# Gate stores of a hybrid encoder layer: issued by ScalarE's queue instead of SyncE's

## Chip, cores and metric

The kernel runs on one NeuronCore of one Trainium2 chip. The metric is the time on the device in microseconds (us) of one execution; the number compared is the median over several executions. Engines are named as in the profile: PE is TensorE's matmuls, PEld its weight loads, DVE is VectorE, ACT is ScalarE, POOL is GpSimd, SP is SyncE. A name with a q (SPq, ACTq) is the sequencer of that engine, where it waits or issues a transfer.

## The reference, cut to what matters

One encoder layer is applied to two batches with the same weights: a prompt of 512 tokens and a sample of 1024 tokens, both 1024 wide, all in float32.

```python
def encoder_layer(x, norm_g, w_in, qn_a, kn_a, rpb_a, qn_b, kn_b, sink_b, w_o_a, w_o_b, w_out, t5_table):
    h = rmsnorm(x, norm_g)
    proj = h @ w_in
    qa, ka, va, za, qb, kb, vb, zb, ga, gb = jnp.split(proj, np.cumsum(SPLITS)[:-1], axis=-1)
    ...
    oa = neighbourhood_attention(qa, ka, va, rpb_a) * jax.nn.silu(za)
    oa = oa @ w_o_a
    ...
    ob = window_gqa_attention(qb, kb, vb, t5_table, sink_b) * jax.nn.silu(zb)
    ob = ob @ w_o_b
    merged = jax.nn.sigmoid(ga) * oa + jax.nn.sigmoid(gb) * ob
    return x + merged @ w_out
```

The two gates sigmoid(ga) and sigmoid(gb), each 1024 wide, are what most of the stores in question hold.

## The kernel before, in words

**Arithmetic.** Every matrix is split into a high and a low part (`split`, L1168: ScalarE makes the rounded high part, VectorE or GpSimd the difference), and every product is three matmuls: high by high, low by high, high by low. That is why nearly all work lies on PE.

**Stages.** In order of time: norm and attention of the prompt (up to about 222 us), the dense stage of the prompt (to about 400 us), attention of the sample (to about 790 us), the dense stage of the sample (to the end). A dense stage (`dense_phase`, L1139) computes z (with silu, times the attention result: `post_z`, L1524), the gates ga and gb (sigmoid: `post_gate`, L1587), the two branch products with the merge, and the output projection. Tiles are 128 partitions by 512 columns, 256 KB each. In the sample's dense stage pairs of columns go through Strassen's scheme (`pair_strassen`, L1349), in the prompt's through plain products (`pair_classic`, L1332).

**What goes through memory outside the core.** SBUF can't hold the gates until the merge, so they are stored to `g_d` and loaded again (L1729). The products of silu(z) with attention go through `u_d` in the sample. All these stores are recorded by one helper, `store` (L1518), whose transfer is issued on L1520:

- kind "u" (`post_z`): the tile is the product that VectorE or GpSimd made last.
- kind "g" from `post_gate`: the tile `C`, on which ScalarE has just applied sigmoid (L1513).
- kinds "g" and "p" from `fill_gates` (L1592): some gate products are computed early, between the matmuls of the attention stages, to fill gaps of PE. Their result leaves PSUM by `leave` (L1612, copy on L1616) into the tile `fc`, of which there is one. The copy may be done by ScalarE or by VectorE: the planner chooses. "p" is the first Strassen product, kept in `p_d` and loaded on L1389.

**What sets the order.** The program is not written in the order in which it runs. Each step is recorded as an operation (`op`, L162) with a choice of engines and a cost in ns on each, a priority, the operations it must follow and the buffers it takes. `run` (L207) then plays a list scheduler over these costs: whenever an engine is free in its model, it takes the ready operation with the smallest priority number, and emits its instructions. So the costs fix the order on every engine's queue, in which instructions then run strictly in turn. A transfer is an operation on SP:

```python
    def dma(self, emit, nbytes, prio, **kw):
        return self.op((("sp", 470),), lambda e: emit(), prio, lag=nbytes / 360, **kw)
```

It takes 470 ns of SP in the plan, and `lag` is the transfer itself. All transfers of the kernel are issued by SP. The priority of the early gate work is -5 for stores, ahead of everything else of the stage.

Of the kernel before, what the change touches and what calls it, by code (L numbers as in the profile page):

```python
# [140 lines left out]
class Flow:  # L141
# [45 lines left out]

    def dma(self, emit, nbytes, prio, **kw):
        return self.op((("sp", 470),), lambda e: emit(), prio, lag=nbytes / 360, **kw)

    def stage(self, prio, close=(), open=(), make=()):

        ends = [o for o in self.ops if any(v.args[0] in close for v in o.vals)]
        for v in make:
            v.held = True

        def emit(e):
            for p in close:
                p.close()
            for p in open:  # L200
                p.open()
            for v in make:
                v.make()

        return self.op((("sp", 0),), emit, prio, after=ends)
# [149 lines left out]
def encoder_kernel(  # L355
# [23 lines left out]
    nc = tc.nc  # L379
    act = nc.scalar  # L380
# [51 lines left out]
    f = Flow(pspool)  # L432
# [706 lines left out]
    def dense_phase(geo, hh, hl, h_ops, o_stores, exps_done, start, opened, tp, up, p0, p1, p2, x_t, y_t, classic, fill, after_gates=None, side=None):  # L1139
# [21 lines left out]
        dma = f.dma  # L1161
# [74 lines left out]
        def stored_sums(prio, d, after):  # L1236

            tv, ops = {}, {}
            for j in (1, 2, 0, 3):
                tv[j] = tuple(f.value(tp, [P, 4, nh], F32R, "T", 8) for _ in range(2))  # L1240
                vh, vl = tv[j]
                for k in range(4):
                    st = spare(("fh", "w32")[k // 2]) if not short and d is t_d and k % 2 else tile_("U", 4)
                    dma(
                        lambda st=st, j=j, k=k: nc.sync.dma_start(st.t[:, :nh], d[j, k]), 512 * nh, prio, new=[st],
                        after=[*after(j, k), *([opened] if d is t_d else [])],
                    )
                    ops[j, k] = split(
                        lambda vh=vh, k=k: vh.t[:, k], lambda vl=vl, k=k: vl.t[:, k], lambda st=st: st.t[:, :nh], nh, prio,
                        (vh, k == 0), (vl, k == 0), [st],  # L1250
                    )
            return moving_sums(tv, ops)


        def load_raw(src, prio):
            v = tile_("raw", 4, 512)
            dma(lambda: nc.sync.dma_start(v.t, src), 262144, prio, new=[v], after=[start])
            return v
# [58 lines left out]
        def weight_sums(i, raw, ends, prio):  # L1317
            o = None
            for j, out, in0, in1, op in (
                (2, (1, 1), (1, 0), (1, 1), ALU.add), (1, (1, 0), (0, 0), (1, 0), ALU.subtract),  # L1320
                (0, (0, 0), (1, 1), (0, 0), ALU.subtract), (3, (0, 1), (0, 1), (0, 0), ALU.subtract),
            ):
                v, a, b = raw[out], raw[in0], raw[in1]
                o = tt(
                    lambda v=v: v.t, lambda a=a: a.t, lambda b=b: b.t, op, 512, prio, hold=[v, a, b],
                    after=[*ends, *([o] if o else [])],
                )
                s_saves[i, j] = dma(
                    lambda v=v, j=j: nc.sync.dma_start(s_d[i, j], v.t), 262144, prio, after=[o], hold=[v],
                )  # L1330
# [185 lines left out]
            return sg  # L1516

        def store(kind, key, dst, v, n, prio):  # L1518
            stores.setdefault((kind, *key), []).append(
                dma(lambda: nc.sync.dma_start(dst, v.t[:, :n]), 512 * n, prio, use=[v])  # L1520
            )


        def post_z(c, a, n, v, in_psum, prio):  # L1524
            sg = sigmoid(v, n, prio, not in_psum, AF.Silu)
            m = n // nb
            ots = [tile_("ot", n_ot) for _ in range(2 if c >= 4 else 1)]
            for e, ot in enumerate(ots):
                if c < 4:
                    src, dst = o_d[nt][e, c, :, a : a + n], lambda ot=ot: ot.t[:, :n]  # L1530
                else:
                    src = o_d[nt][e, c].rearrange("p (i n) -> p i n", n=P)[:, :, a // nb : a // nb + m]
                    dst = lambda ot=ot: ot.t[:, :n].rearrange("p (i n) -> p i n", n=m)
                dma(
                    lambda dst=dst, src=src: nc.sync.dma_start(dst(), src), 512 * n, prio - 0.5, new=[ot],
                    after=o_stores[c, a // nh],
                )
            ot, ov, sv = ots[0], lambda: ots[0].t[:, :n], lambda: sg.t[:, :n]
            if len(ots) > 1:
                tt(ov, ov, lambda: ots[1].t[:, :n], ALU.add, n, prio, use=ots, into=[ot])  # L1540
            if c < 4:
                tt(sv, sv, ov, ALU.mult, n, prio, use=[sg, ot], into=[sg])
            else:
                gv = lambda: sv().rearrange("p (n i) -> p n i", n=m)
                tt(gv, gv, lambda: ov().rearrange("p (i n) -> p n i", n=m), ALU.mult, n, prio, use=[sg, ot], into=[sg])
            if short:
                split_u(c, a, n, sg, prio)
            else:
                store("u", (c, a // nh), u_d[c, :, a : a + n], sg, n, prio)
# [37 lines left out]
        def post_gate(br, m, a, n, v, in_psum, prio):  # L1587
            store("g", (br, m, a // nh), g_d[br, m, :, a : a + n], sigmoid(v, n, prio, not in_psum), n, prio)
# [3 lines left out]
        def fill_gates(prio):  # L1592
# [5 lines left out]
            for br, m in filled if short else filled[::2]:  # L1598
# [13 lines left out]
                def leave(ps, kind, key, dst):  # L1612
                    v = f.value(wpool, [P, nh], F32, "fc", 1)
                    o = f.op(
                        (("act", ACT_(nh, False)), ("dve", DVE_(nh))),
                        lambda e, v=v, ps=ps: act.activation(v.t, ps.t, AF.Copy) if e == "act" else dve.tensor_copy(v.t, ps.t),  # L1616
                        soon, new=[v], use=[ps], port=False,
                    )
                    store(kind, key, dst, v, nh, prio)
                    return o  # L1620
# [22 lines left out]
        for i in range(0 if short else 4):  # L1643
# [5 lines left out]
                use=[ps],  # L1649
# [58 lines left out]
        for q in range(8):  # L1708
            m = q if short else q // 2 + 4 * (q % 2)
            prio = 12 + q  # L1710
# [4 lines left out]
            for n in halves:  # L1715
                gs_ = []
                for br in range(2):
# [14 lines left out]
                    if (br, m) in filled and (short or (m % 2, n) == (0, 0)):  # L1732
# [3 lines left out]
                        use=[ps, g], into=[g],  # L1736
# [213 lines left out]
```

## Time and profile before

| | |
|---|---|
| median of 3 runs | 1136.74 us (1136.4 to 1139.61) |
| the profiled execution | 1139.25 us, of it 1137.5 us in the profile's span |
| granted TensorE clock, mean over the span | 0.998 |
| stores issued on L1520 | 72: 34 `g_d<-C`, 14 `g_d<-fc`, 8 `p_d<-fc`, 16 `u_d<-C` |
| moved by all transfers | 186.11 MB, mean 164 GB/s |

The profile is one execution. Its views are: busy time by engine, busy time of each engine in chosen stretches of the span (a table by stage), who waited for whom (a row has the waiting engine and line, what ended the wait, the total in us, how many times, and the longest), the chain of waits that ended last, the instructions in order of time, and the instructions of one line. An issue of a transfer isn't counted as busy time of its engine. Matmuls overlap, so the duration of one (0.39 us for 512 columns) is longer than the distance from one start to the next.

### The profile page before, as it was taken

What the parts mean: (1) busy time and instruction counts of PE and PEld (TensorE: products, weight loads), DVE (VectorE), ACT (ScalarE), POOL (GpSimd) and SP (SyncE); (2) the same over time, 40 slices, a digit from 0 to 9 for tenths busy, and PEclk for the clock granted to TensorE, in tenths of its full rate; (3) what the DMA queues carried; (4) which work ended last, traced back from release to release, by engine and by line L of the source; (5) the groups of instructions that cost most, each with busy time, mean ns of one, the idle gap of its engine ahead of it and who ended that gap; (6) DMA issues with size and microseconds to landing.
All of it is one profiled execution on the core that took longest, in us unless ns stands there. A gap on an engine that the chain in (4) does not pass through costs nothing.

```text
span 1137.5 us, 18703 instructions
## 1 busy us (share of the span) xinstructions
PE 1121.8 (99%) x6079; PEld 975.1 (86%) x6079; DVE 856.8 (75%) x1988; ACT 651.4 (57%) x1499; POOL 339.3 (30%) x438
## 2 busy tenths in 40 slices
PE   8999999999999999999999999999999999999998
PEld 6999988888888889999999988988788888888877
DVE  5878797587776568787878889876988766767564
ACT  5777987644532247565769888877543435333430
POOL 3654433000011144434324343510333323123111
PEclk9999999999999999999999999999999999999999
DMA  7854543488785743121213214244888645756862
GB/s 257 273 159 138 185 115 103 107 254 257 246 286 202 249 138 91 29 61 29 82 41 93 73 38 119 50 131 138 288 261 237 206 158 191 278 197 224 262 208 93
DMA packets 139108, 186.11 MB, mean 164 GB/s; under 512 B 29897, under 2 KB 68561, under 8 KB 139010
## 3 DMA queue, kind: packets, MB, share of 16 engines
q1 hardware_dynamic: 139010, 184.91, 51.8%
q8 instruction: 48, 0.79, 0.3%
q14 instruction: 50, 0.41, 0.1%
HBM read 137.66 MB, written 51.92 MB: 167 GB/s over the span
## 4 chain that ended last, share of the span: by engine, by line
PE 90%; DMA 4%; DVE 2%; ACT 1%; issue 1%; SPq 1%; POOL 0%; ACTq 0%; DVEq 0%
PE p L764 26%; PE x L1293 8%; PE x L1295 8%; PE x L1294 8%; PE x L1066 5%; PE x L1029 5%; PE x L937 5%; PE p L1294 4%; PE p L1295 4%; PE p L1293 4%; PE d L1293 4%; PE d L1295 4%; PE d L1294 4%; PE x L864 2%; DMA w<-in_w_att_dram 1%; DMA U<-m_d 1%
## 5 line engine op out<-in xcount | busy, mean ns | idle before, releaser
L764 PE MATMUL p<-whi,hh 128*128 128x384 f32 x384 | 133.7, 348 | 0.0
L764 PE MATMUL p<-whi,hl 128*128 128x384 f32 x384 | 132.6, 345 | 0.0
L764 PE MATMUL p<-wlo,hh 128*128 128x384 f32 x384 | 132.0, 344 | 0.0
L1172 ACT ACTIVATE whi<-raw 128x512 fp32r<-128x512 f32 (+1 forms) x140 | 81.5, 600 | 73.0 <-PE x L1294 22.5
L981 ACT ACTIVATE sb<-sb,mx 128x384 f32<-128x384 f32 (+1 forms) x192 | 107.7, 565 | 16.9 <-DVE mx L972 16.6
L1294 PE MATMUL x<-T,whi 128*128 128x512 f32 x280 | 108.9, 389 | 0.0
L1293 PE MATMUL x<-T,whi 128*128 128x512 f32 x280 | 108.9, 389 | 0.0
L1295 PE MATMUL x<-T,wlo 128*128 128x512 f32 x280 | 108.9, 389 | 0.0
L764 PE MATMUL p<-whi,hb 128*128 128x384 f32 x384 | 107.6, 346 | 0.0
L1177 DVE TENSOR_TENSOR wlo<-raw,whi 128x512 fp32r<-128x512 f32 (+1 forms) x110 | 73.4, 678 | 34.5 <-ACT whi L1172 31.0
L1177 POOL TENSOR_TENSOR wlo<-raw,whi 128x512 fp32r<-128x512 f32 (+1 forms) x30 | 36.4, 1219 | 210.2 <-ACT whi L1172 210.2
L1040 DVE TENSOR_TENSOR pp<-x,pp 128x512 fp32r<-128x512 f32 (+1 forms) x136 | 82.6, 639 | 19.2 <-ACT pp L1035 18.5
L802 POOL TENSOR_TENSOR rs_r<-rs_v,mhalf 128x4 f32<-128x4 f32 (+1 forms) x72 | 80.7, 1121 | 5.7
L1293 PE MATMUL x<-hh,whi 128*128 128x512 f32 x200 | 78.4, 392 | 2.1 <-ACT fh L1440 2.1
L1035 ACT ACTIVATE pp<-x 128x512 fp32r<-128x512 f32 (+1 forms) x136 | 70.9, 561 | 15.2 <-PE x L1029 14.0
L1295 PE MATMUL x<-hh,wlo 128*128 128x512 f32 x200 | 78.5, 393 | 0.0
L1294 PE MATMUL x<-hl,whi 128*128 128x512 f32 x200 | 78.3, 392 | 0.0
L1066 PE MATMUL x<-pp,v 128*128 128x256 f32 (+1 forms) x368 | 75.8, 322 | 0.0
L764 PEld LDWEIGHTS p<-whi,hl 128*128 128x128 f32 x384 | 72.8, 190 | 1.3 <-issue 1.0
L764 PEld LDWEIGHTS p<-wlo,hh 128*128 128x128 f32 x384 | 73.0, 190 | 1.0 <-issue 0.7
L764 PEld LDWEIGHTS p<-whi,hh 128*128 128x128 f32 x384 | 73.0, 190 | 0.7 <-DVE v L812 0.3
L764 PEld LDWEIGHTS p<-whi,hb 128*128 128x128 f32 x384 | 69.1, 188 | 3.0 <-issue 1.3
(388 smaller groups left out, 2967.8 us busy)
## 6 DMA issues: line engine op xcount, KB each, us to landing
raw<-in_w_g_dram SPq DMA_DIRECT2D x84, 256.0 KB
w<-in_w_att_dram SPq DMA_DIRECT2D x46, 384.0 KB
raw<-in_w_z_dram SPq DMA_DIRECT2D x40, 256.0 KB
ot<-o_d SPq DMA_DIRECT2D x36, 256.0 KB
g_d<-C SPq DMA_DIRECT2D x34, 256.0 KB
fr<-in_w_g_dram SPq DMA_DIRECT2D x28, 256.0 KB
raw<-in_w_out_dram SPq DMA_DIRECT2D x28, 256.0 KB
out_dram<-C SPq DMA_DIRECT2D x19, 256.0 KB
```

Of the source, the lines that this page charges most:

```text
L764: pe.matmul(ps.t[:, :GW], part[u](k), mv.t[:, c], start=k == 0 and m == 0, stop=k == KC - 1 and m == 2,)
L802: lambda e: nc.gpsimd.tensor_tensor(r.t[:, :nn], rv.t[:, :nn], mhalf[:, :nn], op=ALU.pow),
L937: pe.matmul(pss[2 * pair + i].t[:, :width], q.t[rows, u, at : at + P], kv[:, tiles[0] : tiles[-1] + 1 : step], start=n == 0, stop=n == 2,)
L981: act.activation(sb.t[:, :width], sb.t[:, :width], AF.Exp, bias=mx.t[:, i : i + 1], scale=-1.0, accum_out=sm.t[:, i : i + 1],)
L1035: lambda e, pt=pt, pp=pp, nn=nn: act.activation(pp.t[:, 0, :nn], pt.t[:, :nn], AF.Copy),
L1040: lambda e, pt=pt, pp=pp, nn=nn: dve.tensor_tensor(pp.t[:, 1, :nn], pt.t[:, :nn], pp.t[:, 0, :nn].bitcast(F32), op=ALU.subtract),
L1066: pe.matmul(out(), v.t[:, vs], mv(), start=first, stop=last)
L1172: (("act", ACT_(n)),), lambda e: act.activation(hi(), src(), AF.Copy), prio,
L1177: lambda e: engines[e].tensor_tensor(lo(), src(), hi().bitcast(F32), op=ALU.subtract), prio,
L1293: pe.matmul(out, hi.t[:, cs], mh(), start=first and k == 0, stop=False, **more)
L1294: pe.matmul(out, hi.t[:, cs], ml(), start=False, stop=False, **more)
L1295: pe.matmul(out, lo.t[:, cs], mh(), start=False, stop=last and k == len(ws) - 1, **more)
```

## The change

Stores of the kinds "g" and "p" are issued by ScalarE's own queue, at 430 ns of ScalarE in the plan instead of 470 ns of SP. Kind "u" and every load stay on SP. Nothing is added to or taken from what is computed or moved.

```diff
     def dma(self, emit, nbytes, prio, **kw):
         return self.op((("sp", 470),), lambda e: emit(), prio, lag=nbytes / 360, **kw)
+
+    def act_dma(self, emit, nbytes, prio, **kw):
+        return self.op((("act", 430),), lambda e: emit(), prio, lag=nbytes / 360, **kw)
...
         def store(kind, key, dst, v, n, prio):
+            put, queue = (dma, nc.sync) if kind == "u" else (f.act_dma, act)
             stores.setdefault((kind, *key), []).append(
-                dma(lambda: nc.sync.dma_start(dst, v.t[:, :n]), 512 * n, prio, use=[v])
+                put(lambda: queue.dma_start(dst, v.t[:, :n]), 512 * n, prio, use=[v])
             )
```

## The prediction

> **What bounds the kernel now.** I read the table by stage first: it says how much of the end the change can reach at all.
>
> ```profile
> core 0 of [0], span 1137.5 us
> core 0: us, PE busy (x) PEld busy (x) DVE busy (x) ACT busy (x) POOL busy (x), PEclk, DMA share, GB/s
> 0.00:70.00 70.00, 63.89 (x366) 57.45 (x367) 49.64 (x146) 47.40 (x108) 35.80 (x56) 1.00 0.75 256
> 70.00:222.00 152.00, 151.98 (x949) 135.63 (x948) 121.30 (x349) 119.48 (x300) 56.87 (x92) 1.00 0.43 126
> 222.00:320.00 98.00, 98.00 (x435) 81.12 (x434) 72.20 (x152) 44.20 (x78) 0.00 (x0) 1.00 0.82 253
> 320.00:540.00 220.00, 217.50 (x1262) 196.21 (x1261) 160.03 (x405) 110.18 (x274) 72.48 (x99) 1.00 0.40 130
> 540.00:780.00 240.00, 239.78 (x1527) 215.22 (x1526) 200.01 (x561) 191.39 (x478) 82.57 (x118) 1.00 0.28 77
> 780.00:870.00 90.00, 88.49 (x393) 72.55 (x392) 75.94 (x111) 41.94 (x82) 24.95 (x18) 1.00 0.82 249
> 870.00:1080.00 210.00, 210.00 (x928) 173.91 (x927) 145.09 (x223) 85.49 (x160) 57.00 (x46) 1.00 0.66 219
> 1080.00:1137.50 57.50, 52.18 (x234) 42.98 (x232) 32.62 (x50) 11.30 (x22) 9.68 (x9) 0.97 0.45 153
> ```
>
> The first number after a stretch is its length, the second PE's busy time. From 70 us to 1080 us PE is busy 1005.75 of 1010 us; in 222 to 320 and in 870 to 1080 us it has no idle time. Only the first 70 us (6.11 us idle) and the last 57.5 us (5.32) have more than 3 us. PE is the bound, so what counts next is who made PE wait after 70 us:
>
> ```profile
> PE x L1293 <- ACT fh L1440: 2.1, 1, 2.1
> PE x L864 <- DVE qk L819: 1.9, 1, 1.9
> PE d L1294 <- DVE T L1177: 1.3, 1, 1.3
> PE p L1293 <- ACT whi L1172: 0.5, 1, 0.5
> PE d L1293 <- ACT fc L1616: 0.2, 1, 0.2
> PE p L1294 <- DVE T L1177: 0.2, 1, 0.2
> ```
>
> That is the whole list: 6.2 us, six waits, none of them ended directly by a transfer. The longest has a price beyond its 2.1 us, which the chain of waits shows (start, length, what):
>
> ```profile
> 1080.04 4.75 DMA U<-m_d
> ...
> 1085.34 0.59 ACT fh L1440
> ...
> 1088.31 0.43 PE x L1294
> ...
> 1091.05 0.23 PE p L1295
> ```
>
> ScalarE sat behind a load of `m_d`, PE behind ScalarE; afterwards matmuls came every 0.43 us instead of every 0.23 until about 1090.5. The table's clock of 0.97 in this last stretch says the same: 3% of 57.5 us, about 1.7 us lost. The wait thus cost 2.1 + 1.7 = 3.8 us.
>
> **What is removed.** These are the issues of the line in question, with their lengths in ns, shortest, median and longest:
>
> ```profile
> L1520 SPq DMA_DIRECT2D g_d<-C x34: 319/326/577, 266.0 to 970.8; - x34
> L1520 SPq DMA_DIRECT2D u_d<-C x16: 320/428/3495, 792.7 to 879.4; - x16
> L1520 SPq DMA_DIRECT2D g_d<-fc x14: 319/330/553, 71.0 to 782.0; - x14
> L1520 SPq DMA_DIRECT2D p_d<-fc x8: 326/332/531, 444.6 to 776.5; - x8
> ```
>
> 34 + 14 + 8 = 56 stores leave SP, at 0.33 us each 18.5 us of issuing. More goes with them, because SP stood still for the writers of the stored tiles, and every load behind it stood too:
>
> ```profile
> SPq L1257 <- DVE wlo L1177: 61.0, 48, 3.4
> SPq L1520 <- ACT fc L1616: 50.5, 13, 13.7
> SPq L1520 <- ACT C L1513: 43.2, 26, 4.0
> ...
> SPq L1520 <- DVE fc L1616: 4.7, 2, 3.5
> ```
>
> Part of the third row belongs to "u" stores, so SP loses at most 50.5 + 43.2 + 4.7 = 98.4 us of standing. But the first row shows what is late next: the weight loads of L1257 wait themselves for their buffer, 61.0 us in 48 waits, and a load can't go before its buffer is free. Where the waits for stores lie, PE lacks nothing: all 34 "C" stores lie in the stretches of 222 to 320 and 870 to 1080 us, where PE's idle time is 0.00. A load that comes sooner there is worth nothing. Value on the path: 0 there, and elsewhere at most the share of the 6.2 us that hangs on a load.
>
> Bandwidth doesn't change: the same bytes move. The Trainium skill, "DMA: Bandwidth & Descriptors", section "Issuing engines are not separate DMA queues", says that transfers started by different engines run on the same 16 DMA engines, and that issuing from several saves only the sequencer's time. By that rule too the gain is SP's 18.5 us and no more; no run here shows it yet.
>
> **What is added.** Each store now stands in ScalarE's queue and waits there for its writer. Two neighbours before:
>
> ```profile
> 664.88 0.60 ACT L1616 ACTIVATE fc<-d 128x512 f32<-128x512 f32 x1
> 665.38 0.62 ACT L1172 ACTIVATE fh<-fr 128x512 fp32r<-128x512 f32 x1
> ```
>
> ScalarE starts the next operation 0.50 us after the start of one that takes 0.60, so it overlaps 0.10 us. A store in between waits for the end: 0.10 us of overlap lost plus 0.33 us of issuing, 0.43 us a store. The trace has no issue on ScalarE, so that is an estimate. From below, 0.33 us (nothing lost but the issue; a gain is excluded, since ScalarE gives up no work). From above, 0.58 + 0.10 = 0.68 us with the longest issue of a moved kind. I take 0.43, as the medians of all three kinds are at 0.33. For 56 stores that is 24 us of ScalarE (18 to 38).
>
> By stage: 24 "C" stores are 10.3 us in 870 to 1080, where ScalarE is idle 124.5 us; 10 are 4.3 us in 222 to 320, with 53.8 idle. The "fc" stores fall where ScalarE is fullest:
>
> ```profile
> L1520 SPq DMA_DIRECT2D g_d<-fc x7: 326/332/332, 541.8 to 771.3; - x7
> L1520 SPq DMA_DIRECT2D p_d<-fc x7: 326/332/531, 602.4 to 776.5; - x7
> ```
>
> ```profile
> 597.00:683.00 86.00, 85.78 (x551) 77.67 (x551) 74.31 (x206) 76.70 (x178) 36.65 (x48) 1.00 0.25 67
> ```
>
> These are the issues between 540 and 780 us, 14, and the fullest part of that stretch by the table's columns. 14 stores are 6.0 us of ScalarE against 48.6 idle. From 597 to 683 us ScalarE is idle 9.3 of 86 us; at the stage's density five stores fall there, 2.2 us. What queues behind such a store is what the attention feeds PE with: exponentials, the high parts of the probabilities, the copies out of PSUM. Cover: those 9.3 us, and PE's stock of early gate products. If the cover were gone, all 22 "fc" stores would come through, 22 x 0.43 = 9.5 us.
>
> A second wait is new. The copy on L1616 isn't always ScalarE's:
>
> ```profile
> L1616 ACT ACTIVATE fc<-d x16: 597/598/607, 133.0 to 781.4; 128x512 f32<-128x512 f32 x16
> ...
> L1616 DVE COPY fc<-d x6: 667/692/692, 70.3 to 746.5; 128x512 f32<-128x512 f32 x6
> ```
>
> For 6 of 22, ScalarE now waits for VectorE. The planner puts the store in only when, by its costs, the copy is done; the wait is how far VectorE runs behind the plan. The nearest row is SP's: 4.7 us in 2 waits for the six, 0.8 us each, the longest 3.5. I take 0.8, so 4.7 us of ScalarE, between 0 and 6 x 3.5 = 21 us.
>
> **The new order.** The planner's costs change, so from the first moved store, planned for about 70 us, the order on all queues may differ. PE's work is the same and a ready matmul is always preferred to idling, so this moves only the waits at the seams of the stages: the idle 2.50 us in the stretch from 320, 1.51 in that from 780, and the 3.8 us just worked out before 1086 us. Each may go, stay, or come up elsewhere. From the rows I can't sign it, so I take 0.
>
> **Sum.** Against the profiled execution of 1139.25 us (span 1137.5, 1.75 around it): removed 0, added 0 through cover of ScalarE's idle time, plus perhaps 0.3 us for the fullest stretch. That execution is 2.5 us above the median of 1136.74, within the runs' spread to 1139.61. Carried to the median: 1136.74 + 0.3 = 1137.0 us.
>
> **The rivals.** About 0.3%, or 3.4 us, is what a measurement of this kernel can tell from no change.
>
> *Faster: SP's freedom reaches the seams.* Loads issued sooner shorten the waits that hang on them. For it: the wait before 1086 us goes back to a load, and SP stood 98 us for stores. Against it: the last moved store is issued at 970.8 us, 115 us ahead of that seam. In reach after 70 us are 6.2 us of waits and 1.7 us of clock: 1136.7 - 7.9 = 1128.8 us at the best, with half of it 1132.8 us. The Trainium skill, "Perfetto Trace Analysis", section "DMA Optimizations", recommends one issuing engine for loads and another for stores. By that rule this would be the likelier way; the rows with PE idle 0.00 speak against.
>
> *Slower: the store holds ScalarE in the attention.* Place: the 22 "fc" stores, with probabilities and copies behind them. It decides where the delay passes the time by which ScalarE runs ahead of PE; the row of PE waiting 0.2 us for the copy on L1616 shows that this lead can be nil. If half of the 9.5 us comes through, 1136.7 + 4.8 = 1141.5 us; all, 1146.2 us. The price of one store rises if its issue is held up as the "u" store's 3495 ns was on SP. The Trainium skill, "Perfetto Trace Analysis", section "DMA Instruction — HWDGE (DVE, Sync)", says that the two sequencers which issue such transfers share one descriptor generator, locked for the time of an issue. By that rule an issue on ScalarE can also wait for SP's; with all issues on one queue, this trace can't show it.
>
> *Slower by a new seam.* The new order leaves one more wait like that before 1086 us: 1136.7 + 3.8 = 1140.5 us.
>
> *Not what it says.* For the 6 stores of VectorE's copies the writer isn't ScalarE. Priced above at 4.7 us of ScalarE; with half of it on the path 1136.7 + 2.4 = 1139.1 us, still within no change.
>
> **Numbers.** No measurable change: 0.49, at 1137.0, within 1133.3 to 1140.1. Faster: 0.24, mostly 1129 to 1133. Held ScalarE: 0.15, 1140.5 to 1146. New seam: 0.12, 1140.2 to 1144. The range 1131.0 to 1144.0 leaves out about 0.09 below and 0.07 above. The likeliest case alone spans 1133.3 to 1140.1.
>
> **What would show it.** Right: PE's busy time and its idle time by stage as in the table, but for the seams; 56 issues on ScalarE's queue of 0.33 us; SP's waits for L1513 and L1616 all but gone, with longer waits for buffers on L1257 in their place; ScalarE's busy time unchanged at 651 us with shorter idle time. Wrong in the slow direction: waits of PE for L1035, L1073 or L981 between 540 and 780 us, or issues on ScalarE of over 1 us. Wrong in the fast direction: PE's idle time in the stretches from 320, 780 and 1080 us gone.

## The result, and the profile after

The changed kernel takes 1143.78 us (median of 6 runs, 1141.5 to 1144.87), the kernel before took 1138.17 us beside it (6 runs, 1136.4 to 1139.92). The ratio is 1.0045, 95% interval 1.0028 to 1.0062: slower by 5.6 us, and most of the interval lies beyond the 0.3% that the prediction called no change. The prediction started from 1136.74 us for the kernel before, so 1.4 us of its distance to the measured time is the starting point. The profiled execution took 1144.76 us, of it 1143.0 us in the span, against 1137.5 us of span before.

The table by stage of the changed kernel, three of its rows (length, PE, PEld, DVE, ACT, POOL busy with counts, clock, DMA share, GB/s):

```profile
222.00:320.00 98.00, 98.00 (x434) 81.16 (x433) 71.37 (x149) 43.28 (x78) 0.00 (x0) 1.00 0.78 237
320.00:540.00 220.00, 213.47 (x1207) 191.62 (x1206) 155.29 (x386) 106.14 (x262) 70.31 (x96) 0.98 0.42 135
1080.00:1143.00 63.00, 59.13 (x271) 48.93 (x270) 40.26 (x60) 17.09 (x34) 12.15 (x11) 1.00 0.52 179
```

Where the "C" stores of the prompt lie, in 222 to 320 us, PE still has no idle time. The stretch from 320 us has 6.53 us of idle time instead of 2.50, and a clock of 0.98 instead of 1.00. The last stretch has a better clock: 1.00 instead of 0.97. Who makes PE wait in the changed kernel, over the whole span but for one wait of 4.6 us for a load in the first 70 us (of the first row, one wait of 0.5 us lies there too, and 2.7 us after it):

```profile
PE x L867 <- DVE qk L822: 3.2, 4, 1.8
PE x L1296 <- ACT hh L1175: 3.1, 1, 3.1
PE p L1297 <- DVE T L1180: 1.3, 1, 1.3
PE x L1297 <- DVE hl L1180: 0.7, 1, 0.7
PE d L1296 <- ACT fc L1620: 0.7, 1, 0.7
PE x L1296 <- ACT fh L1443: 0.7, 1, 0.7
PE x L1032 <- POOL sb L1014: 0.2, 1, 0.2
```

(The lines from L190 on have moved by 3, those from L1523 on by 4; the store's issue is L1524.) Two rows of over 0.2 us are new: 3.1 us for `hh` and 0.7 us for `hl`, the split of the merged prompt. The rows for `qk` and `fc` were there before, and are longer now. The wait of 2.1 us for `fh` before the end has shrunk to 0.7. The new waits lie at one place, the start of the prompt's output projection; a table around it, of the changed kernel, same columns:

```profile
350.00:359.09 9.09, 6.13 (x26) 4.43 (x24) 7.29 (x12) 2.03 (x4) 2.95 (x2) 1.00 0.55 182
359.09:365.90 6.81, 5.96 (x13) 4.41 (x14) 2.81 (x5) 1.89 (x3) 0.00 (x0) 0.50 0.78 217
365.90:372.00 6.10, 6.10 (x28) 5.02 (x27) 4.06 (x6) 1.26 (x2) 1.29 (x1) 1.00 0.62 221
```

From within the longer wait on, the clock is 0.50 for 6.81 us. PE works 5.96 us of them, at half speed, so 3.0 us are lost: with the waits of 0.70 and 3.12 us that is 6.8 us in all. The Trainium skill, "TensorE: Matmul & The Clock Gate", section "Part 1: The HAM clock gate", gives the window in which idle time is judged as about 3.4 us. By that the half clock comes in pieces of 3.4 us; the trace agrees (two pieces here, one of 3.4 us from 1087.2 us on in the kernel before).

Why PE waited is read from two times. PE's arrival at the projection (its first `x<-hh`), and the last split of the merge. First the kernel before, the last split on ScalarE and PE's arrival:

```profile
L1172 ACT ACTIVATE hh<-C x1: 633/633/633, 354.2 to 354.2; 128x512 fp32r<-128x512 f32 x1
```

```profile
351.50 0.39 PE L1293 MATMUL x<-hh,whi 128*128 128x512 f32 x1
```

Then the changed kernel:

```profile
359.26 0.63 ACT L1175 ACTIVATE hh<-C 128x512 fp32r<-128x512 f32 x1 [4.54 <-DVE C L1169]
```

```profile
350.93 0.39 PE L1296 MATMUL x<-hh,whi 128*128 128x512 f32 x1
```

PE arrives 0.6 us sooner than before, the last split comes 5.0 us later. I call the distance of the two *lateness*: 2.7 us before, 8.3 us after, each read in one execution; how far it moves from one execution to the next isn't known. The merge was late from its first product on, which waits for the first gate that is loaded back (before, then after):

```profile
319.03 0.69 DVE L1166 TENSOR_TENSOR C<-x,C 128x512 f32<-128x512 f32 x1 [3.32 <-DMA C<-g_d]
```

```profile
323.32 0.69 DVE L1169 TENSOR_TENSOR C<-x,C 128x512 f32<-128x512 f32 x1 [5.03 <-DMA C<-g_d]
```

The stores themselves do what was said of them:

```profile
L1524 ACTq DMA_DIRECT2D g_d<-C x34: 326/327/356, 268.6 to 978.7; - x34
L1524 ACTq DMA_DIRECT2D g_d<-fc x14: 326/326/341, 71.7 to 797.1; - x14
L1524 ACTq DMA_DIRECT2D p_d<-fc x8: 326/326/336, 453.1 to 791.4; - x8
```

The question for the runs: is the lateness made by the queue that issues the stores (theory of the queue), or by the order that the planner made of the new costs (theory of the order)? And is it what costs the 5.6 us?

### The profile page after: what moved, and what is told of

Same layout as the page of the kernel before. It is cut to its first block, busy times and chain, and to the rows that moved or that the text cites. A ratio compares the mean times of both kernels' runs of the same rounds, so it can differ in the third digit from the quotient of the medians.

```text
span 1143.0 us, 18634 instructions
## 1 busy us (share of the span) xinstructions
PE 1125.0 (98%) x6079; PEld 977.3 (86%) x6079; DVE 861.5 (75%) x1978; ACT 653.2 (57%) x1499; POOL 339.7 (30%) x448
## 4 chain that ended last, share of the span: by engine, by line
PE 81%; DMA 6%; DVE 6%; issue 3%; ACT 2%; SPq 1%; POOL 1%; DVEq 0%; POOLq 0%; ACTq 0%
PE p L767 25%; PE x L1296 7%; PE x L1297 7%; PE x L1298 7%; PE x L1069 5%; PE x L940 5%; PE x L1032 5%; PE d L1296 4%; PE d L1298 3%; PE d L1297 3%; PE p L1297 3%; PE p L1298 3%; PE p L1296 3%; DMA xt<-in_xt_s_dram 2%; PE x L867 2%
```

## The experiments

In the table, "loss at 350" is PE's waits of over 0.2 us between 350 and 372 us plus half of PE's busy time at half clock there; "five seams" adds the same for 372 to 395, 395 to 425, 800 to 830 and 1080 to 1100 us. These columns are from the one profiled execution of each kernel, the median and the ratio are from all its runs, against runs of the kernel before on the same chip. "Order" is read from the traces: the sequence of matmuls on PE and of operations on VectorE, ScalarE and GpSimd. Where only PE's is the same, the column says so.

| kernel | order | lateness | loss at 350 | five seams | span | median | ratio, 95% |
|---|---|---|---|---|---|---|---|
| before | old | 2.7 | 0.0 | 7.8 | 1137.5 | | |
| changed | new | 8.3 | 6.8 | 12.6 | 1143.0 | 1143.78 | 1.0045 [1.0028, 1.0062] |
| e1 | as changed | 9.2 | 6.4 | 11.3 | 1142.4 | 1143.55 | 1.0062 [1.0041, 1.0084] |
| e2 | old | 6.0 | 2.0 | 7.9 | 1138.8 | 1138.4 | 1.001 [0.9996, 1.0024] |
| e3 | PE as changed | 5.6 | 3.3 | 8.1 | 1138.3 | 1144.21 | 1.0062 [1.0042, 1.0083] |
| e4 | PE as before | 4.7 | 0.7 | 5.7 | 1136.8 | 1137.81 | 1.0008 [0.9996, 1.002] |
| e5 | old, fills before the merge | 10.6 | 7.7 | 11.8 | 1142.8 | 1143.21 | 1.0069 [1.0051, 1.0087] |
| e6 | as changed | 8.0 | 6.1 | 8.6 | 1139.0 | 1142.58 | 1.0064 [1.0044, 1.0083] |
| e7 | a third | 5.1 | 1.0 | 5.3 | 1136.9 | 1140.21 | 1.0041 [1.002, 1.0061] |
| e8 | a fourth | 5.7 | 3.4 | 9.6 | 1146.1 | 1143.55 | 1.0072 [1.0048, 1.0096] |
| e9 | as changed, shorter merge | 6.1 | 3.5 | 5.6 | 1136.0 | 1138.78 | 1.0013 [0.9994, 1.0031] |
| e10 | old, fills at 244 us | 9.1 | 6.8 | 10.4 | 1142.2 | 1145.09 | 1.0056 [1.0036, 1.0077] |
| e11 | old | 3.8 | 0.0 | 7.8 | 1137.4 | 1137.33 | 0.9993 [0.9978, 1.0007] |
| e12 | a fifth | 5.5 | 1.5 | 8.1 | 1140.8 | 1143.65 | 1.0045 [1.0028, 1.0062] |

Three things stand in it. The loss at 350 follows the lateness: none up to 3.8 us, 0.7 to 3.5 us from 4.7 to 6.1, and 6.1 to 7.7 us from 8 on. Span less the five seams is 1129.6 to 1132.7 us in every row but that of e8 (1136.5, where PE was already 3 us late at 222 us): most of what differs between these profiles is at the seams. But below 8 us the lateness doesn't tell the time: at 4.7 to 6.1 us e2, e4 and e9 are as fast as before, and e3, e7, e8 and e12 are slower by 0.4 to 0.7%. It accounts for the changed kernel, e1, e5, e6 and e10, and not for these four.

The granted clock is known for every execution, rounded to 0.001. By it half clock costs the changed kernel 3.2 us on the mean of 6 executions and the kernel before 0.7 us on the mean of 65: nearly half of the 5.6 us is clock, the rest is time at full clock. The seven executions of e7 stand at 0.999 to 1.0, so half clock isn't what e7 loses.

**e1: the new order, the stores on the old queue.** In the trace the order of operations on PE, VectorE, ScalarE and GpSimd is that of the changed kernel, operation by operation.

```diff
-            put, queue = (dma, nc.sync) if kind == "u" else (f.act_dma, act)
+            put, queue = (dma, nc.sync) if kind == "u" else (f.act_dma, nc.sync)
```

> Order theory: the time is lost in the order that the planner makes from the new costs, whichever queue issues. PE, DVE and POOL run the changed kernel's order here, only the issue goes back to SP: 1143 us (1141 to 1145), with PE idle about 4 us in 355 to 360 us again and the half clock after it. Queue theory: ScalarE's issues cost the time; then this is back at 1138 us (1136.5 to 1139.5) with no wait of PE near 358 us.

Measured: 1143.55 us, 1.0062. PE's waits of e1:

```profile
PE x L1296 <- ACT hh L1175: 3.6, 2, 3.1
PE p L1297 <- DVE T L1180: 2.0, 1, 2.0
PE x L867 <- DVE qk L822: 1.6, 2, 1.1
PE x L1297 <- DVE hl L1180: 0.8, 1, 0.8
```

The same wait of 3.1 us for the same split, with not one store on ScalarE's queue. The loss comes with the order.

**e2: the old order, the stores on the new queue.**

```diff
+            put, queue = (dma, nc.sync) if kind == "u" else (dma, act)
-                dma(lambda: nc.sync.dma_start(dst, v.t[:, :n]), 512 * n, prio, use=[v])
+                put(lambda: queue.dma_start(dst, v.t[:, :n]), 512 * n, prio, use=[v])
```

> Order theory: the old order with issues on ScalarE stays at 1138 us (1136.5 to 1139.5), ScalarE's next operation 0 to 0.46 us later behind each of the 56 issues, no wait of PE in 340 to 370 us. Queue theory: 1143 us (1141 to 1145).

Measured: 1138.4 us, 1.001 with an interval that holds 1. On all four engines the order is that of the kernel before. The queue by itself, taken over the whole kernel, costs and gains nothing that can be measured here. It isn't without effect at the seam: in this profile the first merge product starts at 322.78 us instead of 319.03, the lateness is 6.0 instead of 2.7 us, and 2.0 us are lost at 350; the last seam loses 0.3 instead of 3.8. So the queue can make the merge late too, only not as late as the new order with the old queue (9.2 us in e1).

**e3 and e4: half the change each.** e3 moves only the stores of `fc`, e4 only those of `C`, both with the new price. They were meant as two more orders. The traces show otherwise: PE runs e3 in the order of the changed kernel and e4 in the order of the kernel before, matmul for matmul, and on the other engines some 30 operations stand elsewhere. The price of the 22 `fc` stores alone makes the new order.

```diff
+            put, queue = (dma, nc.sync) if v.tag != "fc" else (f.act_dma, act)
```

> Only the 22 stores of the tile fc move. Queue theory: these are the ones beside the attention, so most of the loss, 3 to 5.6 us, 1141 to 1144 us. Order theory: a third order, whose time hangs on the seams alone: without a wait of PE near 358 us 1135 to 1140 us, with it 1141 to 1145; the six of the prompt come before that seam, so it can be there.

> Only the 34 stores of the tile C move. Queue theory: ScalarE is 45% idle or more there, so little, 1138 to 1139.5 us. Order theory: a fourth order; if the lateness before 358 us is made in 222 to 315 us, where ten of these stores lie, the wait is here and the time 1141 to 1145 us, else 1135 to 1140.

Measured: e3 1144.21 us (1.0062), e4 1137.81 us (1.0008). The profiled execution of e3, 1140.1 us, was its shortest, so its row understates the loss. e3 moves 22 stores, has the changed kernel's order on PE, and loses as much as the whole change; e11, below, moves the same 22 in the old order and loses nothing; e4 moves the other 34 and keeps the old order on PE, and loses nothing either. Again it is the order.

**e5: the old order and queue, the merge made late.** 36 small fills of an unused tile on VectorE ahead of the second head group's first product:

```diff
+        def late(ps, hold):
+            for _ in range(36 if hold else 0):
+                dve.memset(left_pad, 0.0)
+            return ps.t
...
-                        lambda g=g: g.t, lambda ps=ps: ps.t, lambda g=g: g.t, ALU.mult, nh, prio, psum=True,
+                        lambda g=g: g.t, lambda ps=ps, hold=short and q == 1 and br == 0: late(ps, hold), lambda g=g: g.t,
```

> The kernel before with its own order and its own queue; only 36 small fills of an unused tile on VectorE are put ahead of the second head group's first gate product of the prompt's merge, so that the merge runs some 4 us late (the lateness that the trace of after shows), with nothing else moved. They are work added on VectorE; no result depends on them. Theory (the loss is the merge reaching the prompt's output projection late): PE waits some 3 to 4 us for the last piece near 356 to 360 us, half clock follows for 3 to 7 us, and the time is 1142 to 1146 us. Rival (the lateness is taken up by slack, and the loss has its cause elsewhere in the new order): PE waits less than 2 us there, no half clock, 1137 to 1139.5 us.

Measured: 1143.21 us, 1.0069. A fill came every 0.18 us, so the dose was 6.5 us and not 4; the lateness was 10.6 us. PE's waits of e5:

```profile
PE x L1293 <- ACT hh L1172: 4.9, 2, 3.1
PE x L864 <- DVE qk L819: 1.6, 1, 1.6
PE d L1294 <- DVE T L1177: 1.5, 1, 1.5
PE x L1293 <- ACT fh L1440: 1.0, 1, 1.0
PE x L1294 <- DVE hl L1177: 0.8, 1, 0.8
```

The kernel before, made late at this one place, shows the changed kernel's waits, 6.8 us of half clock and its time, at a lateness 2.3 us greater.

**e6: a repair that didn't repair.** In the changed kernel the loads of the gates stand behind `t_d<-xt` stores in SP's queue; these went to ScalarE's queue.

```diff
-                lambda j=j, dst=dst: nc.sync.dma_start(
+                lambda j=j, dst=dst: nc.scalar.dma_start(
```

> The changed kernel in its own order; only the 16 stores of the normed tiles' sums (t_d<-xt, one line) are issued by ScalarE's queue as well, while the planner still books them on SP. Theory (in the changed kernel the reloads of the gate results stand behind such stores in SP's order, the merge starts late from that, and the seam pays): the first reload into C is issued 2 to 3 us earlier than 317.3 us, the first merge product starts near 320 to 321 us instead of 323.3, PE's wait near 360 us falls from 3.1 to about 1 us, and the time is 1138 to 1141 us. Rival (the reloads wait for something else, the stores' landing or the buffers of C): no reload earlier by over 1 us, 1143 to 1145 us. A third outcome, that ScalarE stands at these stores waiting for VectorE's xt and delays its own splits, would show as ScalarE waits and no gain.

Measured: 1142.58 us, 1.0064; the first load into `C` was issued at 320.77 us instead of 317.34, later and not sooner. It was the third outcome. What ScalarE waited for in e6 between 305 and 326 us:

```profile
ACT hh L498 <- DVE xt L491: 8.2, 2, 7.0
ACT C L1516 <- DVE xt L586: 2.5, 1, 2.5
ACT hh L498 <- DVE wlo L1180: 2.2, 1, 2.2
ACT whi L1175 <- DMA t_d<-xt: 1.7, 1, 1.7
```

The second row is a sigmoid held for 2.5 us by VectorE's `xt`, which it doesn't read: the store ahead of it in the queue does. This is the price of a store that isn't behind its own writer, and it tells nothing of what makes the loads late.

**e7 and e8: new orders with no change of queue.** The kernel before, with the planned price of a transfer on SP at 471 and at 460 ns.

```diff
-        return self.op((("sp", 470),), lambda e: emit(), prio, lag=nbytes / 360, **kw)
+        return self.op((("sp", 471),), lambda e: emit(), prio, lag=nbytes / 360, **kw)
```

> The kernel before, queues as they are; only the planner's price for a transfer on SP is 471 ns instead of 470. This changes the planned order on every engine and nothing else, so it shows how far the time moves when the order is drawn anew without any change of queue. If the loss of the changed kernel is one draw among many, this differs from the kernel before by up to 6 us either way (1133 to 1145 us), by PE's waits and the half clock at the seams near 356, 410, 818 and 1086 us, and by nothing inside the stages. If the kernel's order is robust and the changed kernel lost by something particular to its edit, this stays within 1.5 us of the kernel before.

> As the run with 471 ns, with 460 ns: a second draw of the order, no queue changed. One draw among many: anywhere from 1133 to 1145 us, and the two draws differ from each other by over 2 us with the sum of PE's waits and half clock accounting for the difference. Robust order: within 1.5 us of the kernel before.

Measured: 1140.21 us (1.0041) and 1143.55 us (1.0072). One nanosecond in the plan costs about as much as the change under study. The two differ from each other by 3.3 us, with intervals that overlap; PE's order is the same in both up to 420 us. e7's profiled execution has a span as short as that of before, and with less lost at the five seams; what its longer executions lose isn't shown by it.

**e9: the changed kernel with less work in the merge.**

```diff
+                    c = 64 if short and br else nh
-                        lambda g=g: g.t, lambda ps=ps: ps.t, lambda g=g: g.t, ALU.mult, nh, prio, psum=True,
+                        lambda g=g, c=c: g.t[:, :c], lambda ps=ps, c=c: ps.t[:, :c], lambda g=g, c=c: g.t[:, :c], ALU.mult, nh, prio, psum=True,
...
-                    lambda v=v: v.t, lambda a=a: a.t, lambda b=b: b.t, op, 512, prio, hold=[v, a, b],
+                    lambda v=v: v.t[:, :64], lambda a=a: a.t[:, :64], lambda b=b: b.t[:, :64], op, 512, prio, hold=[v, a, b],
```

> The changed kernel in its own order on every engine, stores on ScalarE's queue, but with less VectorE work in the prompt's merge and at its end: the second gate product of each head group (ot<-ot) and the four weight sums of each pair are computed on 64 of their 512 columns; the other columns are left out. Dependencies and instruction counts stay. By the rows of the changed kernel each cut product frees about 0.45 us of VectorE, 8 of them and 3 sums some 4 to 5 us. Theory (the merge is late against PE, and only that lateness costs): the last split starts 3 to 5 us nearer to PE's arrival than the 8.3 us of the changed kernel, the loss at 350 to 372 us falls from 7.2 to at most 2 us, and the time is 1137 to 1140 us though queue and order are the changed kernel's. Rival (the loss sits in the store's issue on ScalarE or elsewhere in the new order): the loss moves or stays, 1142 to 1145 us.

Measured: 1138.78 us, 1.0013 with an interval that holds 1. The time is what the theory said; the working was half right. The lateness fell by 2.2 us and not by 3 to 5, and 3.5 us of loss were left where at most 2 were expected. PE's waits of e9 after 70 us, all of them:

```profile
PE p L1297 <- DVE T L1180: 2.1, 1, 2.1
PE x L1296 <- ACT hh L1175: 1.5, 1, 1.5
PE d L1296 <- ACT fc L1620: 0.7, 1, 0.7
PE x L1297 <- DVE hl L1180: 0.2, 1, 0.2
```

The waits for `qk`, 2.7 us after 70 us in the changed kernel, are gone too, with the half clock behind one of them. This is 3.9 us of the 7.0 us by which the five seams shrank, against 3.4 us at 350, and it can't be put down to the merge: of the 24 operations that were shortened, 12 are weight sums at 366 to 394 us, behind the merge and ahead of those waits. The same cut in the kernel before wasn't timed, so how much it would win there isn't known; by its profile, which loses nothing at 350 and 1.9 us near 412, it would be some 2 us at these two places. What e9 shows is that queue and order of the changed kernel do not by themselves cost time: with less work for VectorE and GpSimd in 320 to 395 us most of the loss is gone.

**e10: a control that wasn't one.** The 36 fills of e5, at 244 us instead of 325.

```diff
-                tt(ov, ov, lambda: ots[1].t[:, :n], ALU.add, n, prio, use=ots, into=[ot])
+                tt(lambda: early(ov, short and c == 4), ov, lambda: ots[1].t[:, :n], ALU.add, n, prio, use=ots, into=[ot])
```

> Control for the run with fills ahead of the merge: the kernel before, its order and its queue, with the same 36 fills of an unused tile on VectorE, put some 110 us before the output projection (ahead of a sum of the prompt's first projection near 244 us), where VectorE has idle time behind. Theory (lateness costs only at a seam where PE finds nothing else to do): 1135.5 to 1138.5 us, no new PE wait over 1 us and none near 356 us. Rival (6.6 us more on VectorE costs wherever it is put): 1141 to 1145 us as with the fills ahead of the merge.

Measured: 1145.09 us, 1.0056. By its time the rival won. But the profile shows the loss at the old place, 3.1 us for `hh` up to 362.6 us and 6.8 us of half clock. The delay had travelled. The last split of e10, and PE's arrival in it:

```profile
L1172 ACT ACTIVATE hh<-C x3: 629/631/632, 351.6 to 361.9; 128x512 fp32r<-128x512 f32 x3
```

```profile
352.81 0.39 PE L1293 MATMUL x<-hh,whi 128*128 128x512 f32 x1
```

The last split is 7.7 us later than in the kernel before, PE only 1.3. VectorE ran 5.9 us behind the kernel before at 245 us, 6.3 at 310, and 7.7 at 354: nothing was regained in 110 us, though VectorE is busy only 72.20 of the 98 us up to 320. The rest wasn't spare time for this delay. What VectorE waited for between 222 and 350 us, the largest row, before and in e10:

```profile
DVE xt L488 <- DMA xt<-in_xt_s_dram: 11.2, 2, 5.8
```

```profile
DVE xt L488 <- DMA xt<-in_xt_s_dram: 11.5, 2, 5.9
```

And what SP's weight loads waited for between 222 and 320 us, before and in e10:

```profile
SPq L1257 <- DVE wlo L1177: 20.3, 17, 3.4
```

```profile
SPq L1257 <- DVE wlo L1177: 20.8, 18, 3.2
```

VectorE waits for loads, the loads wait for VectorE to free their buffers, and both rows are as long in a run that is 6 us late. The reading is that this ring of loads, splits and freed buffers keeps its own pace, and that a delay put into it comes out at its end. PE doesn't feel it, until it reaches the first thing that it can't do ahead of the ring. Both doses, of e5 and of e10, lie ahead of the same seam; one with no such seam behind it wasn't tried.

**e11: the old order, only the `fc` stores on the new queue.**

```diff
-                dma(lambda: nc.sync.dma_start(dst, v.t[:, :n]), 512 * n, prio, use=[v])
+                dma(lambda: (act if v.tag == "fc" else nc.sync).dma_start(dst, v.t[:, :n]), 512 * n, prio, use=[v])
```

> The kernel before in its own order, only the stores of the 22 copies fc issued on ScalarE's queue; the stores of C stay on SP. A version that might beat both: the fc stores stand near the last seam, where the traced run of before lost 3.8 us, and the order that loses at 356 us isn't taken. Queue theory (SP's freedom is worth something at the last seam): 1132 to 1135.5 us. Order theory (the queue is worth nothing in the same order): within 1.5 us of before, 1135 to 1139 us.

Measured: 1137.33 us, 0.9993: no gain, as the theory of the order says. No run found a version faster than the kernel before.

**e12: the store at a lower price.**

```diff
-        return self.op((("act", 430),), lambda e: emit(), prio, lag=nbytes / 360, **kw)
+        return self.op((("act", 200),), lambda e: emit(), prio, lag=nbytes / 360, **kw)
```

> The changed kernel with the planner's price of a store on ScalarE lowered from 430 to 200 ns, near the mean of what the trace of the changed kernel shows (about 0 behind another activation, about 0.5 us directly behind its writer). A new order again. If the price was the fault, 1136 to 1139 us. If the new order is one draw among many, as the two draws with other prices for SP suggest, it is anywhere from 1136 to 1146 us, more likely over 1139, and the time again follows the lateness of the merge's last split against PE's arrival: under 5 us no loss at 350 to 372 us, at 8 us some 7 us.

Measured: 1143.65 us, 1.0045. The price wasn't the fault. Its profiled execution lost only 1.5 us at 350, and 1.5, 2.2 and 2.4 us at three other seams.

## Why the prediction was right and wrong

The forecast was 1137.0 us and no measurable change; 1143.78 us came out, 0.2 us inside the range. The likeliest case is wrong. The case that came true is the new seam, with a chance of 0.12, and that the range still holds the time is luck: that case was priced at 3.8 us, from another seam.

*PE is the bound; the removed work is worth 0.* Right. SP's waits for ScalarE at the stores are gone, and buffers took their place, as said; of the changed kernel:

```profile
SPq L1260 <- DVE wlo L1180: 83.9, 50, 7.4
```

61.0 us before. In the old order the whole queue change measures 1.001 (e2), so SP's 18.5 us of issuing and its standing bought nothing. The standing was greater than the 98.4 us given as the most: one more row of the kernel before, `SPq L1520 <- DVE qk L819: 16.8, 2, 9.6`, belongs to two `p_d<-fc` stores. It changes nothing on a path where standing is worth 0.

*0.43 us of ScalarE a store.* The size was off both ways. With another activation between writer and store, in the changed kernel:

```profile
307.15 0.58 ACT L1516 ACTIVATE C<-d 128x512 f32<-128x512 f32 x1
307.63 0.62 ACT L1175 ACTIVATE whi<-raw 128x512 fp32r<-128x512 f32 x1
307.76 0.33 ACTq L1524 DMA_DIRECT2D g_d<-C  x1
308.15 0.62 ACT L498 ACTIVATE hh<-xt 128x512 fp32r<-128x512 f32 x1
```

The issue runs while `whi` runs, and the next activation starts 0.52 us after `whi`, the usual distance: the store costs nothing. Right behind its writer it costs more:

```profile
889.63 0.63 ACT L1516 ACTIVATE C<-C 128x512 f32<-128x512 f32 x1 [1.70 <-DVE C L1169]
890.29 0.33 ACTq L1524 DMA_DIRECT2D g_d<-C  x1
890.72 0.64 ACT L1175 ACTIVATE whi<-raw 128x512 fp32r<-128x512 f32 x1 [0.46 <-ACT C L1516]
```

The next one starts 1.09 us after the writer instead of the 0.52 of the rows above, so the store costs nearly 0.6 us. Of the changed kernel's 56 stores 16 start right behind their writer; at 0.57 us that is 9 us, less than the 24 us estimated, and e2 shows that none of it reaches the end.

*4.7 us of waiting for VectorE's copies.* The row behind it was misread. The two `p_d<-fc` stores just named start 0.03 us behind VectorE's copies, at 683.1 and 718.2 us, so SP's wait for those copies was at least 4.7 + 16.8 = 21.5 us in 4 waits, the longest 9.6. In the changed kernel ScalarE waited for such a copy once, 0.6 us at 758.7 us; its other stores of VectorE's copies were issued 0.7 to 9.8 us behind them.

*Held ScalarE in the attention; issues held up.* Neither came. Between 540 and 780 us PE is idle 0.81 us, and 0.22 before. No issue on ScalarE took over 0.36 us in the changed kernel, and none over 0.61 us in the other runs (e6). The Trainium skill's rule of a shared descriptor generator ("Perfetto Trace Analysis", section "DMA Instruction — HWDGE (DVE, Sync)") would show as long issues on ScalarE; these rows show none, while SP's longest in the kernel before took 3.5 us.

*Faster through separate queues for loads and stores.* The Trainium skill's recommendation ("Perfetto Trace Analysis", section "DMA Optimizations") is tried in part by e2 and e11 in the old order, with 56 and 22 of the stores on another queue than the loads: 1.001 and 0.9993, both intervals holding 1. So far it neither helps nor harms this kernel.

*"This moves only the waits at the seams of the stages: the idle 2.50 us ... 1.51 ... and the 3.8 us ... I can't sign it, so I take 0."* This is the step that failed, in two ways. It listed only the seams at which PE waited, and not the one at 350 us, where PE did not: there the kernel before was 2.7 us late, and the profiles put the edge between 3.8 and 4.7, so between 1 and 2 us stood between it and a loss. And it took a new order to be as likely better as worse. On PE four orders other than the old one were timed here: that of the changed kernel (also in e3), and those of e7, e8 and e12. All four are slower, by 0.4 to 0.7%; the runs that keep the old order on PE and add no work (e2, e4, e11) are the same as before. The new orders aren't four independent draws, since e7 and e8 share theirs up to 420 us. Still, none is faster, and every one of their profiles has a greater lateness than before's 2.7 us (as e2 and e4 have too, without a longer time). A kernel that stands at the good end of what its planner can produce is more likely to lose than to win by a new order. The margin at the seam can be read blind, from the time of the last split and PE's arrival. The changed kernel's order begins to differ later than thought: up to 148 us PE, VectorE and ScalarE run the same operations in the same order, and between 222 and 360 us PE still runs the old order, while VectorE and ScalarE don't.

*The price of a new seam, 3.8 us.* It came from another seam. Here it was 6.8 us, since the wait was longer and brought 6.8 us of half clock. With 1.9 us more near 412 us and 3.1 us less at the last seam, five seams cost 12.6 instead of 7.8 us: 4.8 of the span's 5.5 us.

**Open.** What in the new order makes the ring late: VectorE's weight splits fall behind the kernel before by 0.4 us near 238, 2.3 near 267 and 4.3 near 320 us, in no single step, and e6 didn't get at it. What e3, e7, e8 and e12 lose, whose lateness is no greater than that of e2 and e9. That the ring has no spare pace is read from e10's waits; more buffers weren't tried. The time of e8 outside the seams, and why executions of one kernel differ by 5 to 8 us, aren't explained.

## What to carry to other kernels

A cost given to a planner is an edit of every queue: before crediting or blaming a change of queue, run the old order with the new queue and the new order with the old one, and compare the emitted orders before counting a changed cost as a new one. At each seam read how far the last input lies behind the arrival of the engine that sets the time, also where that engine doesn't wait yet, and take this margin as what a new order can use up. Idle time of an engine inside a ring of loads, splits and buffers need not be slack: in e10 a delay put there arrived whole at the ring's end.

## What the runs showed of the hardware

An issue of a transfer on ScalarE's queue runs beside the activation before it: 0.33 us that cost nothing if that activation isn't the writer, nearly 0.6 us if it is.

Waits of PE of 1.4 to 2.3 us were followed by half clock in some profiles and not in others (1.94 us without, 2.09 us with 3.4 us of it, both in the kernel before), while each of the five waits of 3.12 us, in the changed kernel, e1, e5, e6 and e10, came with 6.8 us of it, beginning 0.2 to 2.3 us into the wait.
